# Row sums of 64 MB: two row blocks instead of four, a chained pair sum for the last row, and a first load of one row and of fifteen

## The chip, the cores and the metric

The kernel runs on one core of a Trainium2 chip. The metric is device time in microseconds (us). The kernel before takes 162.77 us (median of 3 runs, 162.54 to 163.09). Four names recur: SP (SyncE) only issues DMA transfers here, DVE (VectorE) and ACT (ScalarE) compute, and ACT also issues some stores. A transfer "lands" when its completion is signalled; a "packet" is one record of the profile for what one of the 16 DMA engines moved in one piece. The profiled span (from the first to the last instruction) is shorter than the device time by about 1.8 us: 161.3 us against 163.13 us for the same execution of the kernel before.

## The reference

```python
x = np.random.randn(32, 512, 1024).astype(np.float32)   # 67.1 MB
out = np.sum(x, axis=-1).astype(np.float32)             # 64 KB
```

That is 16,384 rows of 1024 numbers: each of the 128 partitions gets 128 rows.

## The kernel before

The rows are cut into four blocks; within a block a partition holds 32 consecutive rows, so neighbouring partitions lie 128 KB apart in memory (this distance is called the pitch below). SP issues loads of 16 rows per partition (8 MB, 64 KB in one run per partition) into three buffers. DVE reduces each buffer in one instruction. ACT issues a block's store as soon as its sums are there. The last 16 rows come in smaller loads and are shared between DVE and ACT.

```python
BLOCKS = (32, 32, 32, 32)
G = 16
ACT_ROWS = 6
CUT = 640
...
    xpool = ctx.enter_context(tc.tile_pool(name="x", bufs=3))
...
    for b, n in enumerate(BLOCKS):
        x_b, out_b, res = block(done * P, n)
        final = b == len(BLOCKS) - 1
        whole = n - G if final else n
        c = 0
        while c < whole:
            m = min(G, whole - c)
            xt = xpool.tile([P, G * D], F32, tag="xt", name="xt")
            nc.sync.dma_start(out=xt[:, 0 : m * D], in_=x_b[:, c * D : (c + m) * D])
            a = ACT_ROWS if done + c + m == full else 0
            rows_dve(xt, res, 0, m - a, c)             # one reduction over m - a rows
            rows_act(xt, res, m - a, a, c + m - a)     # one instruction per row
            c += m
        if not final:
            nc.scalar.dma_start(out=out_b, in_=res)    # the early stores
        done += n
    # the last 16 rows: loads of 8, 4, 2 and 1 rows, then the last row in two pieces
    ...
    nc.vector.tensor_reduce(
        out=tail[:, D : D + 1], in_=tail[:, 0 : CUT // 2], axis=X, op=ADD
    )
    sum_act(tail[:, CUT // 2 : CUT], tail[:, D + 1 : D + 2])
    nc.vector.tensor_reduce(
        out=res[:, n - 1 : n], in_=tail[:, CUT : D + 2], axis=X, op=ADD
    )
    nc.sync.dma_start(out=out_b, in_=res)
```

After compilation the first load is moved ahead of the barrier that opens the program. The whole kernel:

## Time and profile before

| | before |
|---|---|
| device time, median | 162.77 us |
| span of the profile | 161.3 us |
| DVE busy | 123.5 us (77%) |
| ACT busy | 15.8 us (10%) |
| bytes moved, mean rate | 67.18 MB, 416 GB/s |

The timeline of the kernel before; columns are start, duration (both us), engine, line, operation, output and input, and in brackets the idle time before it and what ended it. Each large reduction starts within 0.03 us of the landing of its load, so these starts are a list of the landings. "..." stands for lines left out. The line of 58.52 merges the three early stores, which are issued at 58.52, 97.26 and 136.55 us.

```profile
21.93 17.22 DVE L40 TENSOR_REDUCE res<-xt 128x16 f32<-128x16384 f32 x1 [21.93 <-DMA xt<-in_x_dram]
41.27 17.22 DVE L40 TENSOR_REDUCE res<-xt 128x16 f32<-128x16384 f32 x1 [2.13 <-DMA xt<-in_x_dram]
58.52 78.36 ACTq L82 DMA_DIRECT2D out_dram<-res  x3
60.64 17.22 DVE L40 TENSOR_REDUCE res<-xt 128x16 f32<-128x16384 f32 x1 [2.15 <-DMA xt<-in_x_dram]
80.01 17.22 DVE L40 TENSOR_REDUCE res<-xt 128x16 f32<-128x16384 f32 x1 [2.15 <-DMA xt<-in_x_dram]
99.57 17.22 DVE L40 TENSOR_REDUCE res<-xt 128x16 f32<-128x16384 f32 x1 [2.34 <-DMA xt<-in_x_dram]
...
119.30 17.22 DVE L40 TENSOR_REDUCE res<-xt 128x16 f32<-128x16384 f32 x1 [2.51 <-DMA xt<-in_x_dram]
...
138.73 18.46 DVE L40 TENSOR_REDUCE res<-xt 128x10 f32<-128x10240 f32 x4 [2.21 <-DMA xt<-in_x_dram]
...
157.95 0.47 ACT L48 ACTIVATE tail<-tail 128x320 f32<-128x320 f32 x1 [0.97 <-DMA tail<-in_x_dram]
157.95 0.49 DVE L102 TENSOR_REDUCE tail<-tail 128x1 f32<-128x320 f32 x1
...
158.55 0.55 DVE L106 TENSOR_REDUCE res<-tail 128x1 f32<-128x386 f32 x1
159.13 0.35 SPq L109 DMA_DIRECT2D out_dram<-res  x1
```

DVE is always done before the next load lands (17.22 us of work in 19.4 us), so the loads set the pace. Two of the distances between starts are longer than the others: 80.01 to 99.57 is 19.56 us and 99.57 to 119.30 is 19.73 us. At the end, ACT and DVE share the first piece of the last row (from 157.95); the last reduction adds ACT's part, DVE's part and the second piece.

### The profile page before, as it was taken

What the parts mean: (1) busy time and instruction counts of PE and PEld (TensorE: products, weight loads), DVE (VectorE), ACT (ScalarE), POOL (GpSimd) and SP (SyncE); (2) the same over time, 40 slices, a digit from 0 to 9 for tenths busy, and PEclk for the clock granted to TensorE, in tenths of its full rate; (3) what the DMA queues carried; (4) which work ended last, traced back from release to release, by engine and by line L of the source; (5) the groups of instructions that cost most, each with busy time, mean ns of one, the idle gap of its engine ahead of it and who ended that gap; (6) DMA issues with size and microseconds to landing.
All of it is one profiled execution on the core that took longest, in us unless ns stands there. A gap on an engine that the chain in (4) does not pass through costs nothing.

```text
span 161.3 us, 116 instructions
## 1 busy us (share of the span) xinstructions
DVE 123.5 (77%) x14; ACT 15.8 (10%) x29; POOL 0.2 (0%) x4
## 2 busy tenths in 40 slices
DVE  0000059997799959999499994999949998699994
ACT  0000000000000000000000000000000000891881
POOL 0000000000000000000000000000000000000000
DMA  7995995996995995996996996997979969999991
GB/s 260 520 520 260 520 520 260 520 520 260 520 520 260 520 520 260 521 521 260 521 520 260 520 520 260 521 456 326 521 309 471 520 260 520 390 391 449 406 407 44
DMA packets 2448, 67.18 MB, mean 416 GB/s; under 512 B 784, under 2 KB 912, under 8 KB 1168
## 3 DMA queue, kind: packets, MB, share of 16 engines
q1 hardware_dynamic: 2016, 67.13, 97.2%
q10 hardware_dynamic: 432, 0.05, 0.2%
HBM read 67.11 MB, written 0.07 MB: 416 GB/s over the span
## 4 chain that ended last, share of the span: by engine, by line
DMA 76%; DVE 22%; ACT 0%; issue 0%; ACTq 0%
DMA xt<-in_x_dram 39%; DMA tail<-in_x_dram 24%; DVE res L40 21%; DMA out_dram<-res 14%; DVE res L106 0%; ACT tail L48 0%; ACTq L115 0%
## 5 line engine op out<-in xcount | busy, mean ns | idle before, releaser
L40 DVE TENSOR_REDUCE res<-xt 128x16 f32<-128x16384 f32 (+4 forms) x10 | 121.8, 12203 | 35.4 <-DMA xt<-in_x_dram 35.4
L48 ACT ACT_TABLE_LOAD x1 | 1.3, 1283 | 137.0 <-DVE res L40 137.0
L48 ACT ACTIVATE xt<-xt 128x1024 f32<-128x1024 f32 x13 | 13.6, 1045 | 4.8 <-DMA xt<-in_x_dram 4.8
L48 ACT ACTIVATION_READ_ACCUMULATOR xt<-xt 128x1 f32 x13 | 2.4, 186 | 0.0
L56 DVE CUSTOM_DVE_ANT_0 xt<-xt 128x512 f32<-128x512 f32 x1 | 0.7, 692 | 0.0
L106 DVE TENSOR_REDUCE res<-tail 128x1 f32<-128x386 f32 x1 | 0.6, 554 | 0.1
L48 ACT ACTIVATE tail<-tail 128x320 f32<-128x320 f32 x1 | 0.5, 470 | 1.0 <-DMA tail<-in_x_dram 1.0
L102 DVE TENSOR_REDUCE tail<-tail 128x1 f32<-128x320 f32 x1 | 0.5, 486 | 0.0
L48 ACT ACTIVATION_READ_ACCUMULATOR tail<-tail 128x1 f32 x1 | 0.2, 187 | 0.0
L151 POOL MEMSET const-uint8-127<- 128x1 uint8 x1 | 0.1, 103 | 0.0
L151 POOL MEMSET const-bfloat16-1.0<- 128x1 bf16 x1 | 0.1, 102 | 0.0
L151 POOL MEMSET const-float32-0.0<- 128x1 f32 x1 | 0.1, 99 | 0.2 <-issue 0.2
L151 POOL MEMSET const-float32-1.0<- 128x1 f32 x1 | 0.1, 99 | 0.0
L56 DVE DVE_READ_ACCUMULATOR2_ANT res<- 128x1 f32 x1 | 0.1, 84 | 0.0
## 6 DMA issues: line engine op xcount, KB each, us to landing
xt<-in_x_dram SPq DMA_DIRECT2D x1, 4096.0 KB, 31.6
xt<-in_x_dram SPq DMA_DIRECT2D x1, 2048.0 KB, 36.1
xt<-in_x_dram SPq DMA_DIRECT2D x1, 1024.0 KB, 38.1
xt<-in_x_dram SPq DMA_DIRECT2D x1, 512.0 KB, 38.9
tail<-in_x_dram SPq DMA_DIRECT2D x1, 320.0 KB, 38.5
tail<-in_x_dram SPq DMA_DIRECT2D x1, 192.0 KB, 38.6
xt<-in_x_dram SPq DMA_DIRECT2D x7, 41.0
out_dram<-res ACTq DMA_DIRECT2D x3, 16.0 KB, 22.2
```

Source lines behind the costliest of these rows:

```text
L40: nc.vector.tensor_reduce(out=res[:, c : c + n], in_=xt[:, j * D : (j + n) * D].rearrange("p (j d) -> p j d", d=D), axis=X, op=ADD,)
L48: nc.scalar.activation(out=v, in_=v, func=COPY, accum_out=acc)
L56: nc.vector.tensor_tensor_reduce(out=xt[:, a:h], in0=xt[:, a:h], in1=xt[:, h:b], scale=1.0, scalar=first, op0=ADD, op1=ADD, accum_out=acc,)
L102: nc.vector.tensor_reduce(out=tail[:, D : D + 1], in_=tail[:, 0 : CUT // 2], axis=X, op=ADD)
L106: nc.vector.tensor_reduce(out=res[:, n - 1 : n], in_=tail[:, CUT : D + 2], axis=X, op=ADD)
L151: nc = _bacc.Bacc("TRN2", target_bir_lowering=False, num_devices=1)
```

## The change

The intent: fewer stores among the loads (two blocks, so one early store instead of three), a start-up in which a small load goes first, and an end in which DVE alone sums the last row, in two chained pair sums (an operation that adds the two halves of a piece and accumulates), the second of which starts from the first one's result. ACT takes one more whole row instead.

```diff
-BLOCKS = (32, 32, 32, 32)
+BLOCKS = (112, 16)
-CUT = 640
+CUT = 576
+EARLY = 2
...
-            nc.sync.dma_start(out=xt[:, 0 : m * D], in_=x_b[:, c * D : (c + m) * D])
+            parts = (0, 1, m) if done + c == 0 else (0, m)
+            for i, k in zip(parts, parts[1:]):
+                nc.sync.dma_start(
+                    out=xt[:, i * D : k * D], in_=x_b[:, (c + i) * D : (c + k) * D]
+                )
...
-    nc.vector.tensor_reduce(
-        out=tail[:, D : D + 1], in_=tail[:, 0 : CUT // 2], axis=X, op=ADD
-    )
-    sum_act(tail[:, CUT // 2 : CUT], tail[:, D + 1 : D + 2])
-    nc.vector.tensor_reduce(
-        out=res[:, n - 1 : n], in_=tail[:, CUT : D + 2], axis=X, op=ADD
-    )
+    rows_act(xt, res, 14, 1, c + 14)
+    pairs_dve(xt, last, last + CUT, 0.0, part)
+    pairs_dve(xt, last + CUT, last + D, part, res[:, c + 15 : c + 16])
...
-    load = next(i for i in code if i.engine == sp)
+    loads = [i for i in code if i.engine == sp][:EARLY]   # both go ahead of the barrier
```

Besides the number of stores, the blocks change two things: the early store has runs of 448 B instead of 128 B per partition, and neighbouring partitions of the first 112 rows lie 448 KB apart instead of 128 KB.

More of the change, by code (lines that the diff above doesn't have):

```diff
@@ L36, in row_sums @@
     rpool = ctx.enter_context(tc.tile_pool(name="res", bufs=1))
-    tail = rpool.tile([P, D + 2], F32, name="tail")
+    part = rpool.tile([P, 1], F32, name="part")
     def rows_dve(xt, res, j, n, c):
@@ L88, in row_sums @@
         nc.sync.dma_start(out=xt[:, i * D : k * D], in_=x_b[:, (c + i) * D : (c + k) * D])
-    last = (n - 1) * D
-    nc.sync.dma_start(out=tail[:, 0:CUT], in_=x_b[:, last : last + CUT])
-    nc.sync.dma_start(out=tail[:, CUT:D], in_=x_b[:, last + CUT : last + D])
-    for i, k in zip(cuts[:2], cuts[1:3]):
-        h = (k - i + 1) // 2
-        rows_dve(xt, res, i, h, c + i)
-        rows_act(xt, res, i + h, k - i - h, c + i + h)
-    i = cuts[2]
-    rows_dve(xt, res, i, 1, c + i)
-    rows_act(xt, res, i + 1, 1, c + i + 1)
-    i += 2
-    pairs_dve(xt, i * D, (i + 1) * D, 0.0, res[:, c + i : c + i + 1])
-    nc.vector.tensor_reduce(
-        out=tail[:, D : D + 1], in_=tail[:, 0 : CUT // 2], axis=X, op=ADD
-    )
-    sum_act(tail[:, CUT // 2 : CUT], tail[:, D + 1 : D + 2])
-    nc.vector.tensor_reduce(
-        out=res[:, n - 1 : n], in_=tail[:, CUT : D + 2], axis=X, op=ADD
-    )
+    last = 15 * D
+    for i, k in ((0, CUT), (CUT, D)):
+        nc.sync.dma_start(
+            out=xt[:, last + i : last + k],
+            in_=x_b[:, c * D + last + i : c * D + last + k],
+        )
+    for i, k in zip(cuts[:3], cuts[1:4]):
+        h = (k - i) // 2
+        rows_dve(xt, res, i, h, c + i)
+        rows_act(xt, res, i + h, h, c + i + h)
+    rows_act(xt, res, 14, 1, c + 14)
+    pairs_dve(xt, last, last + CUT, 0.0, part)
+    pairs_dve(xt, last + CUT, last + D, part, res[:, c + 15 : c + 16])
     nc.sync.dma_start(out=out_b, in_=res)
@@ L128 @@
     code = list(body.instructions)
-    load = next(i for i in code if i.engine == sp)
-    assert load.opcode == "DMACopy" and not load.sync_info.on_wait
-    code.remove(load)
+    loads = [i for i in code if i.engine == sp][:EARLY]
+    for load in loads:
+        assert load.opcode == "DMACopy" and not load.sync_info.on_wait
+        code.remove(load)
     body.instructions = code
@@ L134 @@
     at = next(k for k, i in enumerate(code) if i.engine == sp and i.opcode == "Drain")
-    code.insert(at, load)
+    code[at:at] = loads
     entry.instructions = code
```

## The prediction

> **What bounds the kernel before.** It is a stream of loads. The page gives 67.18 MB and no compute engine above 77% of the span (DVE 123.5 of 161.3 us). In the list of waits, DVE waits only for loads (35.4 us). In the timeline, DVE starts its seven large reductions at 21.93, 41.27, 60.64, 80.01, 99.57, 119.30 and 138.73 us, each time when a load lands, and then takes 17.22 us, less than the 19.4 us to the next landing. Single packet records show 64 KB per engine in 2.418 us, so 433.6 GB/s over 16 engines; the Trainium skill ("DMA: Bandwidth & Descriptors", "Where 436 GB/s comes from") puts the port ceiling at 435 GB/s, and the trace agrees. So only what is lost around it can shrink. Sixty-four such packets per engine are 154.8 us. First packets start at 0.99 us and the last load lands at 158.4: about 2.7 us are lost, of which the first packets take about 0.75 (3.2 us each instead of 2.42). After that landing come 0.12 us of waiting for ACT's part of the last row, a 0.55 us reduction, then store and closing (159.13 to 161.3).
>
> **What the change does.**
> 1. Three early stores of 128 B runs become one of 448 B runs. The undisturbed period between landings is 19.37 us; the periods with stores in flight are 19.56, 19.73 and 19.43, an excess of 0.6 us for somewhat over two stores, so 0.2 to 0.25 us each (an estimate). Two stores fewer: −0.45 us on the stream.
> 2. The partition stride of the loads goes from 128 KB to 448 KB. Runs stay 64 KB, and the engines already run at the port's rate: 0, with a small risk of a slower memory pattern.
> 3. First load 1 + 15 rows. The reduction stays one instruction over 16 rows, so DVE does not start earlier. The start-up loss is latency that small packets pay too: 0 to −0.4, I take −0.1[...].
> 4. Last row: DVE's reduction over 386 elements, after ACT (0.12 + 0.55 us after the landing), becomes a pair sum over 224 elements without ACT. From the 512-wide pair sum (0.69 us) I estimate about 0.40 us: −0.25.
> 5. A cost on ACT: its only early store now stands between its six rows and its last eight, and waits for DVE's ten-row reduction (10.82 us after the seventh landing), then takes 0.43 us. Eight rows at 1.04 us with a last read then end 19.7 us after the seventh landing, about when DVE's last pair sum ends. Before, ACT started these rows at 148.47, now about 149.4. So this nearly ties with the last landing and may eat 0 to 0.2 us.
>
> Sum: the last store is issued at about 158.4 instead of 159.13. The closing part is unchanged. **Predicted time 161.95 us**, range 161.3 to 162.6: 0.5% less. Chances: faster by over 2% 0.02, within 2% 0.96, slower 0.02.
>
> **What would show it.** Landing periods all close to 19.37 us up to the seventh; seventh landing near 138.1 instead of 138.7; ACT idle in the timeline until about 149 us with its rows then back to back; the last DVE operations about 0.4 us; the last wait shared between ACT's row and the last load.
>
> **What would make it wrong.** A 448 KB stride that slows packets above 2.42 us (slower by several us); a start-up loss that scales with the packet (up to 0.7 us more gain); an ACT tail that ends well after the last landing (up to 0.5 us less gain).

## More of the kernel before

Lines of the page of the kernel before: the span, busy time and its share, and the two DMA queues with packets, MB and the time of their packets as a share of 16 engines' span (q1 carries the loads and the last store, q10 the three early stores).

```profile
span 161.3 us, 116 instructions
...
DVE 123.5 (77%) x14; ACT 15.8 (10%) x29; POOL 0.2 (0%) x4
...
q1 hardware_dynamic: 2016, 67.13, 97.2%
q10 hardware_dynamic: 432, 0.05, 0.2%
```

The load queue takes 97.2% of what 16 engines have; no compute engine comes near.

## The result, and the profile after

| | before | after |
|---|---|---|
| device time, median | 162.66 us (4 runs, 162.46 to 163.09) | 162.32 us (4 runs, 162.26 to 162.56) |
| span of the profile | 161.3 us | 160.5 us |
| DVE, ACT busy | 123.5, 15.8 us | 122.7, 16.0 us |

The ratio after/before is 0.9979, with a 95% interval of 0.9955 to 1.0002. A ratio in this document is the mean time of one kernel's runs over that of the other's of the same rounds, so it isn't quite the ratio of the medians quoted; where a call had more runs of the kernel before than the rounds compared, the median quoted is that of all of them. The verdict is "same": a gain of 0.2%, where 0.5% was predicted.

Lines of the page of the changed kernel, as before:

```profile
span 160.5 us, 118 instructions
...
DVE 122.7 (76%) x14; ACT 16.0 (10%) x29; POOL 0.2 (0%) x4
...
q1 hardware_dynamic: 2160, 67.12, 97.3%
q10 hardware_dynamic: 144, 0.06, 0.1%
```

The timeline of the changed kernel, the lines that answer to those of before, and the early store with what follows it on ACT:

```profile
21.81 17.22 DVE L41 TENSOR_REDUCE res<-xt 128x16 f32<-128x16384 f32 x1 [21.81 <-DMA xt<-in_x_dram]
41.09 17.22 DVE L41 TENSOR_REDUCE res<-xt 128x16 f32<-128x16384 f32 x1 [2.06 <-DMA xt<-in_x_dram]
...
99.14 17.22 DVE L41 TENSOR_REDUCE res<-xt 128x16 f32<-128x16384 f32 x1 [2.13 <-DMA xt<-in_x_dram]
...
118.49 17.22 DVE L41 TENSOR_REDUCE res<-xt 128x16 f32<-128x16384 f32 x1 [2.13 <-DMA xt<-in_x_dram]
137.84 18.46 DVE L41 TENSOR_REDUCE res<-xt 128x10 f32<-128x10240 f32 x4 [2.13 <-DMA xt<-in_x_dram]
...
148.75 0.37 ACTq L87 DMA_DIRECT2D out_dram<-res  x1
149.25 1.06 ACT L49 ACTIVATE xt<-xt 128x1024 f32<-128x1024 f32 x1 [3.70 <-DVE res L41]
...
157.24 0.46 DVE L57 CUSTOM_DVE_ANT_0 xt<-xt 128x288 f32<-128x288 f32 x1 [0.93 <-DMA xt<-in_x_dram]
157.48 0.19 ACT L49 ACTIVATION_READ_ACCUMULATOR xt<-xt 128x1 f32 x1
...
157.77 0.45 DVE L57 CUSTOM_DVE_ANT_0 xt<-xt,part 128x224 f32<-128x224 f32 x1
...
158.29 0.35 SPq L108 DMA_DIRECT2D out_dram<-res  x1
```

At first sight this confirms the prediction handsomely. The distances between the starts from the second on are now all 19.35 us; the seventh load lands 0.89 us earlier (137.84 against 138.73), and the last store is issued 0.84 us earlier (158.29 against 159.13). But the timed runs moved by only 0.34 us, and the experiments show that three early stores can leave the periods unstretched and that periods stretch without any.

### The profile page after: what moved, and what is told of

Same layout as the page of the kernel before. It is cut to its first block, busy times and chain, and to the rows that moved or that the text cites. A ratio compares the mean times of both kernels' runs of the same rounds, so it can differ in the third digit from the quotient of the medians.

```text
span 160.5 us, 118 instructions
## 1 busy us (share of the span) xinstructions
DVE 122.7 (76%) x14; ACT 16.0 (10%) x29; POOL 0.2 (0%) x4
## 4 chain that ended last, share of the span: by engine, by line
DMA 74%; DVE 22%; SPq 1%; issue 0%; DVEq 0%
DMA xt<-in_x_dram 74%; DVE res L41 21%; SPq L93 1%; DVE xt L57 1%; DVEq L57 0%; DVE part L57 0%; DVEq L114 0%
## 5 line engine op out<-in xcount | busy, mean ns | idle before, releaser
L49 ACT ACTIVATE xt<-xt 128x1024 f32<-128x1024 f32 x14 | 14.6, 1042 | 3.7 <-DVE res L41 3.7
L57 DVE CUSTOM_DVE_ANT_0 xt<-xt 128x288 f32<-128x288 f32 x1 | 0.5, 459 | 0.9 <-DMA xt<-in_x_dram 0.9
L57 DVE CUSTOM_DVE_ANT_0 xt<-xt,part 128x224 f32<-128x224 f32 x1 | 0.5, 452 | 0.1
```

The lines of the kernel that those rows point to most:

```text
L49: nc.scalar.activation(out=v, in_=v, func=COPY, accum_out=acc)
L57: nc.vector.tensor_tensor_reduce(out=xt[:, a:h], in0=xt[:, a:h], in1=xt[:, h:b], scale=1.0, scalar=first, op0=ADD, op1=ADD, accum_out=acc,)
```

## The experiments

Twelve runs were made, each on one chip and beside its own runs of the kernel before. All gave the reference's result. Four numbers are read from each profile. "2nd" is the start of the second large reduction; "2nd to 7th" is the distance from there to the start of the seventh, five load periods in which the start-up and the end play no part. "7th to last load" leads on to the landing of the last load (from the semaphore events of the trace), and "to store" from there to the issue of the last store. "Long packets" counts the 64 KB packets of the loads that took over 2.45 us (their median is 2.418 to 2.42 us everywhere; there are 768 or 864 of them after the start).

| run | early stores | 2nd | 2nd to 7th | 7th to last load | to store | long packets | time / before | ratio (95%) |
|---|---|---|---|---|---|---|---|---|
| before | 3 x 128 B | 41.27 | 97.46 | 19.67 | 0.73 | 180 | - | - |
| f1_before_again | 3 x 128 B | 41.15 | 97.20 | 19.71 | 0.72 | 91 | 162.58 / 162.54 | 1.0004 (0.9991 to 1.0018) |
| e3_first_only | 3 x 128 B | 41.17 | 97.32 | 19.70 | 0.73 | 143 | 162.88 / 162.74 | 1.0009 (0.9994 to 1.0024) |
| e1_after_again | 1 x 448 B, late | 41.11 | 97.25 | 19.85 | 0.66 | 93 | 162.53 / 162.74 | 0.9991 (0.9977 to 1.0005) |
| e4_tail_only | 3 x 128 B | 41.31 | 96.81 | 19.67 | 0.66 | 5 | 162.51 / 162.74 | 0.9990 (0.9977 to 1.0003) |
| e5_three_stores | 128, 128, 192 B | 41.03 | 96.85 | 19.71 | 0.66 | 2 | 162.34 / 162.53 | 0.9983 (0.9970 to 0.9997) |
| e7_seven_stores | 7 x 64 B | 41.58 | 96.98 | 19.66 | 0.66 | 22 | 163.07 / 162.53 | 1.0029 (1.0016 to 1.0041) |
| after | 1 x 448 B, late | 41.09 | 96.75 | 19.79 | 0.66 | 16 | 162.32 / 162.66 | 0.9979 (0.9955 to 1.0002) |
| f3_after_third | 1 x 448 B, late | 41.39 | 96.75 | 19.76 | 0.66 | 15 | 162.31 / 162.54 | 0.9992 (0.9979 to 1.0004) |
| e2_blocks_only | 1 x 448 B, late | 41.25 | 96.76 | 19.77 | 0.73 | 9 | 162.58 / 162.74 | 0.9995 (0.9981 to 1.0008) |
| e6_one_block | none | 41.31 | 96.76 | 19.64 | 0.65 | 12 | 162.66 / 162.53 | 1.0002 (0.9989 to 1.0015) |
| e8_store_from_sp | none among the loads | 40.97 | 96.76 | 19.67 | 0.66 | 25 | 162.15 / 162.53 | 0.9978 (0.9962 to 0.9994) |
| f4_sp_store_again | none among the loads | 41.42 | 96.75 | 19.67 | 0.66 | 16 | 162.33 / 162.54 | 0.9989 (0.9976 to 1.0001) |
| f2_before_stores_last | none among the loads | 41.17 | 96.77 | 19.73 | 0.70 | 33 | 162.37 / 162.54 | 0.9997 (0.9985 to 1.0010) |

The theories were: A, the prediction's, that each store among the loads stretches the stream by 0.2 to 0.25 us; P, that the 448 KB pitch is what makes the stream quicker; B, that the stores cost nothing; and, after eight runs, S, that the stretched periods were a stretch of slower packets which comes and goes with the execution.

### e1: the changed kernel again

No edit.

> A repeat of the changed kernel, for the size of the noise and the repeat of its profile. Expected by my accounting: about 0.4 us less than the kernel before (ratio 0.997 to 0.999), seventh landing (the wait that frees the ten-row reduction) again near 137.8 us. If the gain is only chance between chips, the ratio is 1.000 and the landings move by several tenths.

The timed gain was smaller (ratio 0.9991), and the profile differs from the first one of the same kernel. The timeline of this run:

```profile
79.82 17.22 DVE L41 TENSOR_REDUCE res<-xt 128x16 f32<-128x16384 f32 x1 [2.14 <-DMA xt<-in_x_dram]
99.18 17.22 DVE L41 TENSOR_REDUCE res<-xt 128x16 f32<-128x16384 f32 x1 [2.14 <-DMA xt<-in_x_dram]
...
118.72 17.22 DVE L41 TENSOR_REDUCE res<-xt 128x16 f32<-128x16384 f32 x1 [2.32 <-DMA xt<-in_x_dram]
138.36 18.53 DVE L41 TENSOR_REDUCE res<-xt 128x10 f32<-128x10240 f32 x4 [2.42 <-DMA xt<-in_x_dram]
```

The distances are 19.36, 19.54 and 19.64 us, though this kernel's only early store is issued at 149 us, after all of them. So stretched periods arise without any store. The packet records show why: 93 packets of 64 KB took over 2.45 us, the longest 2.67 us, nearly all between 75 and 135 us; in the first profile of the same kernel it was 16, the longest 2.47 us. They are about enough to explain the stretch: between the second and the seventh reduction, what the long packets took beyond 2.418 us sums to 0.57 us per engine in e1, to 0.61 us in the kernel before, to 0.54 in e3 and 0.29 in f1, but to 0.09 us or less in every profile without such a stretch.

### e2, e3, e4: one part of the change at a time, in the kernel before

e2 has only the first hunk's blocks, e3 only the split first load and `EARLY = 2`, e4 only the pair sums and `CUT = 576`:

```diff
e2  -BLOCKS = (32, 32, 32, 32)
    +BLOCKS = (112, 16)
e3  +            parts = (0, 1, m) if done + c == 0 else (0, m)
    ...          (the loads of one and of fifteen rows, both ahead of the barrier)
e4  -    nc.vector.tensor_reduce(...)  sum_act(...)  nc.vector.tensor_reduce(...)
    +    rows_act(xt, res, 14, 1, c + 14)
    +    pairs_dve(xt, last, last + CUT, 0.0, part)
    +    pairs_dve(xt, last + CUT, last + D, part, res[:, c + 15 : c + 16])
```

> The kernel before with only the two blocks (112, 16). Theory A (stores cost the stream about 0.2 us each): landing periods after the first all 19.35 to 19.37 us, seventh landing about 0.6 us earlier than before (138.1), time about 0.4 us lower. Rival B (the stores cost nothing, the changed first load and tail bring the gain): seventh landing 138.7, time as before.

> The kernel before with only the first load split into one and fifteen rows ahead of the barrier. Theory A: first tile complete 0.1 to 0.2 us earlier (21.7 against 21.9), the later periods still stretched to 19.56 and 19.73, time 0.1 to 0.2 us lower. Rival B: 0.4 us lower.

> The kernel before with only the chained pair sums for the last row. Theory A, after the profile: from the last landing to the issue of the last store 0.66 us instead of 0.73, so 0.07 us lower and the time the same within noise. The prediction on record said 0.25 us lower. Rival: without the early gain of the stream, ACT's last rows no longer hold anything up and the full 0.25 us shows.

None of the three ratios is clear of 1. e2 has the quiet periods that theory A expected, but its ratio of 0.9995 is worth only 0.08 us, not 0.4. e4 refutes A outright: it has all three early stores, and no stretched period above 19.43 us. Its timeline:

```profile
60.66 17.22 DVE L40 TENSOR_REDUCE res<-xt 128x16 f32<-128x16384 f32 x1 [2.14 <-DMA xt<-in_x_dram]
80.09 17.22 DVE L40 TENSOR_REDUCE res<-xt 128x16 f32<-128x16384 f32 x1 [2.21 <-DMA xt<-in_x_dram]
99.38 17.22 DVE L40 TENSOR_REDUCE res<-xt 128x16 f32<-128x16384 f32 x1 [2.07 <-DMA xt<-in_x_dram]
...
118.80 17.22 DVE L40 TENSOR_REDUCE res<-xt 128x16 f32<-128x16384 f32 x1 [2.20 <-DMA xt<-in_x_dram]
...
138.12 18.47 DVE L40 TENSOR_REDUCE res<-xt 128x10 f32<-128x10240 f32 x4 [2.10 <-DMA xt<-in_x_dram]
```

The distances are 19.43, 19.29, 19.42 and 19.32 us. "2nd to 7th" is 96.81 us, against 96.75 to 96.77 in every quiet profile without early stores: two stores cost 0.04 to 0.06 us, so 0.02 to 0.03 each. For the tail, e4 gives 0.66 us from last landing to last store where the kernel before has 0.73; every profile with the pair sums has 0.65 or 0.66, and those with the old tail have 0.72 or 0.73 (0.70 in f2). That 0.07 us is the one part of the gain that repeats in every profile. e3 fell into a slow stretch (143 long packets) and its timed runs were not faster than before. Whether the split first load gains anything is not settled: the second reduction starts at 40.97 to 41.42 us in the profiles with the split first load at the 448 KB pitch and at 41.15 to 41.31 us in those without it. The packets hint at a shorter start. With one large load the first packets take 0.62 to 0.75 us more than the usual 2.418, on average over the engines. With the split, an engine's eight packets of 4 KB take 1.63 to 1.89 us instead of eight times 0.159, so 0.36 to 0.61 us more; e6 and e7, at other pitches, are left out here (0.09 and 0.50 us more, but their packets of 60 KB that follow lose another 0.32 and 0.34 us). That is an estimated 0.15 us between the averages, but the tile is complete when its slowest engine is, and there no difference shows.

### e5: three early stores in the changed kernel

```diff
-        if not final:
-            nc.scalar.dma_start(out=out_b, in_=res)
+            if not final and c in (32, 64, 112):
+                k = c - (48 if c == 112 else 32)
+                nc.scalar.dma_start(out=out_b[:, k:c], in_=res[:, k:c])
```

> The changed kernel, its one early store cut into three (columns 0 to 32, 32 to 64, 64 to 112) at the times when the kernel before stores; the partition pitch stays 448 KB. Theory A (each store in the stream costs 0.2 to 0.25 us): the periods in which stores are in flight stretch again to 19.55 to 19.75 us, seventh landing back by 0.4 to 0.6 us to 138.2 to 138.4, time 0.3 to 0.5 us above the changed kernel. Rival P (the 448 KB pitch gives the gain): periods stay 19.35, seventh landing 137.8, time unchanged.

Theory A fails again: 0.3 to 0.5 us were expected on top of the changed kernel, and the ratio to the kernel before is 0.9983, no worse than the changed kernel's 0.9979, 0.9991 and 0.9992. "2nd to 7th" is 96.85 us, 0.10 us over the quiet value for two stores, so 0.05 us each. (The packets of these two stores take 0.21 us per engine, twice what they cost; in e4 it is four times.) "7th to last load" is 19.71 us instead of 19.76 to 19.85: with a store of 192 B runs instead of 448 B the end is shorter. So for the changed kernel it is all the same whether one store or three leave early.

### e6 and e7: the pitch, and no early store or seven

```diff
e6  -BLOCKS = (112, 16)
    +BLOCKS = (128,)
e7  -BLOCKS = (112, 16)
    +BLOCKS = (16,) * 8
```

> The changed kernel with one block of 128 rows: no early store at all, one last store of 512 B runs, partition pitch 512 KB, a large power of two. Theory A: one store fewer in the stream, last landing 0.2 us earlier, last store 0.1 us longer: time 0 to 0.2 us below the changed kernel, packets still 2.42 us. Rival P (pitch matters): packets longer than 2.42 us and the time above by microseconds.

> The changed kernel with eight blocks of 16 rows: seven early stores of 64 B runs, six of them among the first seven loads; pitch 64 KB. Theory A: seventh landing later than in the changed kernel by 6 times 0.2 to 0.25 us, less what the last is still in flight, so 1.0 to 1.5 us, and the time higher by 1.2 to 1.5 us. Rival P: nothing moves that does not follow the pitch; if a smaller pitch is slower, all packets are longer.

The pitch between partitions is 512 KB in e6 and 64 KB in e7. In e6 "2nd to 7th" is 96.76 us, as at 128 KB without stores (f2, 96.77) and at 448 KB (96.75). So rival P falls: the pitch does not move the rate of this stream once it runs. Theory A's expectation for the time was missed too: 0 to 0.2 us below the changed kernel, but the five runs of e6 (162.41 to 162.76 us) all lie above those of e5 (162.26 to 162.37) on the same chip. In the profiles 0.28 us of that stands before the second reduction (41.31 against 41.03). Whether the pitch slows the start is not shown: f3 and f4 start as late (41.39 and 41.42) at 448 KB. The Trainium skill ("DMA: Bandwidth & Descriptors", "Latency and other measured facts") reports that copies between HBM tensors with a row pitch of 512 KiB reach only 207 GB/s per direction. This stream of loads into SBUF in 64 KB runs shows nothing of it, with 2.418 us per packet at 512 KB pitch, that is 433.6 GB/s. The case is not the same as the page's (loads, not copies between HBM tensors; longer runs).

e7 has five stores in flight between the second and the seventh reduction, and "2nd to 7th" is 96.98 us: 0.23 us more than without, so 0.05 us each, where theory A expected 1.0 to 1.5 us for six. Its queue line of the page, to be compared with q10 above:

```profile
q10 hardware_dynamic: 1008, 0.06, 0.4%
```

Its ratio of 1.0029 is worth 0.47 us, and it is the only one clearly above 1. The five stores explain 0.23 us of that at most. Its first load landed late as well (reduction at 22.30 us, elsewhere 21.69 to 22.14), and whether that belongs to the 64 KB pitch was not separated.

### e8 and f4: the early store behind all loads

SP issues the store after all its loads, so it stands in the same ring behind them, and ACT no longer waits.

```diff
-            nc.scalar.dma_start(out=out_b, in_=res)
+            held = out_b, res
...                                   # after the last load is issued
+    nc.sync.dma_start(out=held[0], in_=held[1])
```

> The changed kernel with its early store issued by SP after all loads instead of by ACT between its rows. Theory A (ACT's wait for the ten-row reduction is off the critical path, as its last row ends 0.6 us before the last store): ACT's eight last rows start about 147.5 us instead of 149.25, the last store is issued at the same 158.3 us, time unchanged. Rival (point 5 of the prediction: ACT nearly ties and eats up to 0.2 us): time lower by 0.1 to 0.2 us.

> The changed kernel with the early store issued by SP behind all loads, a second time. Theory S: from the seventh landing to the last load 19.69 us again instead of 19.8, as the 448 B runs (8 packets of 0.025 us per engine) no longer stand among the last loads: time 0.1 to 0.2 us below the changed kernel beside it, ratio to the kernel before 0.997 to 0.998. Rival: no difference between the two.

The timeline of e8, to be read against the end of the changed kernel above:

```profile
147.49 1.06 ACT L49 ACTIVATE xt<-xt 128x1024 f32<-128x1024 f32 x1 [2.05 <-issue]
...
148.61 0.35 SPq L101 DMA_DIRECT2D out_dram<-res  x1
...
157.54 0.45 DVE L57 CUSTOM_DVE_ANT_0 xt<-xt,part 128x224 f32<-128x224 f32 x1
...
158.06 0.34 SPq L110 DMA_DIRECT2D out_dram<-res  x1
```

ACT starts its last rows at 147.49 us, 1.76 us earlier than in the changed kernel, and the time from last landing to last store stays 0.66 us. So the wait of ACT for the ten-row reduction was off the critical path. It cost nothing: ACT had finished at 157.67 us in the changed kernel, 0.62 us before the last store. What did move is "7th to last load": 19.67 us in both e8 and f4, against 19.76 to 19.85 in the four profiles with the late 448 B store. So that one store, among the small last loads, costs about 0.1 us (0.09 to 0.12 in the three quiet profiles, 0.18 in e1). Its packets give an upper bound: each takes 0.025 us, eight per engine, about 0.2 us, where a 128 B packet takes 0.013 us.

In e8 the store issued at 148.61 us lands at 157.61, after the last load (157.40). The Trainium skill ("DMA: Bandwidth & Descriptors", "Queues, rings and completion order") says that an engine consumes one ring's descriptors in order and takes turns between rings packet by packet; the trace, whose packets do not name their engine, fits both. ACT's store at 58.52 us in the kernel before had its 128 B packets spread over the next 64 KB packets, about one per load packet, and landed at 82.40 us, 23.9 us later.

Timed, f4 is 0.05 us below f3 on the same chip (means 162.34 and 162.40), which is not clear of noise. e8 and f4 have ratios of 0.9978 and 0.9989 to the kernel before. This variant may be the quickest by a hair; of the two intervals only e8's is clear of 1, as e5's also is (0.9970 to 0.9997).

### f1, f2, f3: the kernel before, without its stores, and the changed kernel once more

f1 and f3 have no edit. f2 is the kernel before with its stores behind the loads:

```diff
-            nc.scalar.dma_start(out=out_b, in_=res)
+            held.append((out_b, res))
...                                   # after the last load is issued
+    for o, r in held:
+        nc.sync.dma_start(out=o, in_=r)
```

> A repeat of the kernel before, profiled once more. Theory S (the stretched periods of 19.56 and 19.73 us in its first profile were a stretch of slower packets that comes and goes with the execution): about half of such profiles are quiet; if this one is, all packets are near 2.42 us, each period with stores in flight is 19.37 to 19.43, seventh landing near 138.1 to 138.2. Rival A (stores stretch the periods by 0.2 to 0.25 us each): seventh landing 138.7 again with the same two periods stretched.

> The kernel before with its three early stores issued by SP behind all loads, so none in the load stream. Theory S (a store costs what its own packets take, about 0.05 us in the stream for 128 B runs): time 0.1 to 0.15 us below the kernel before, first quiet periods 19.35 us. Rival A: 0.6 to 0.7 us below, seventh landing 138.1 in every profile and no slow packets.

> The changed kernel a third time, to pool its ratio and to stand beside the next one on one chip. Theory S: ratio to the kernel before 0.998 to 0.999; its profile may or may not have slow packets.

The profile of f1 fell into a slow stretch again, but not the same one. Its timeline:

```profile
79.92 17.22 DVE L40 TENSOR_REDUCE res<-xt 128x16 f32<-128x16384 f32 x1 [2.20 <-DMA xt<-in_x_dram]
99.34 17.22 DVE L40 TENSOR_REDUCE res<-xt 128x16 f32<-128x16384 f32 x1 [2.20 <-DMA xt<-in_x_dram]
...
118.94 17.22 DVE L40 TENSOR_REDUCE res<-xt 128x16 f32<-128x16384 f32 x1 [2.37 <-DMA xt<-in_x_dram]
...
138.35 18.47 DVE L40 TENSOR_REDUCE res<-xt 128x10 f32<-128x10240 f32 x4 [2.20 <-DMA xt<-in_x_dram]
```

The period that ends at 99.34 us is 19.42 us (before: 19.56), the next 19.60 (before: 19.73); its seventh landing is 138.35, between the two that S and A named. So for the kernel before a quiet profile is still missing; e4 stands in for it, since its loads and early stores are those of the kernel before until the last row. f2 has a ratio of 0.9997, worth 0.05 us: less than the 0.1 to 0.15 us that S expected and not clear of 1, and far from the 0.6 to 0.7 us of A (its interval ends at 0.9985, worth 0.24 us). f3 repeats the quiet profile of the changed kernel and a ratio of 0.9992.

One thing stays open. The slow stretch appeared in four of the fourteen profiles: three of the six with several early stores among the loads, and one of the eight with one such store or none. So early stores are neither needed for it nor do they always bring it; whether they make it more likely can't be told from so few. What slows the packets in such a stretch no run here shows. The stretch is also not the only scatter: f3's profile is quiet, yet that execution took 162.56 us where three others took 162.28 to 162.31; its second reduction starts at 41.39 us, 0.30 us later than in the first profile of the same kernel. In e8 and f4, again one kernel, it starts 0.45 us apart (40.97 and 41.42).

## Why the prediction was right or wrong, point by point

The predicted time (161.95 us, range 161.3 to 162.6) held the measured 162.32 us, and "within 2%" was right. The size of the gain was not: 0.8 us from the sum, and measured were 0.34, 0.15 and 0.13 us in three comparisons (the ratios 0.9979, 0.9991 and 0.9992, times 162.7 us). Each of the three intervals just includes 1; weighted together by their widths (an estimate) they give 0.9990, 0.9981 to 0.9999, so a gain of about 0.16 us. That the time fell inside the range was partly luck: the largest term of the sum was wrong, and a gain of 0.15 us from the 162.77 us known at the time gives 162.62, just outside.

- **What bounds the kernel: right.** Every quiet profile has its load periods at 19.35 us whatever else is changed (19.29 to 19.43 with stores in flight), and a median packet of 2.418 or 2.42 us.
- **Point 1, stores "so 0.2 to 0.25 us each ... Two stores fewer: −0.45 us": this step failed.** The excess of 0.6 us in the profile before came from a stretch of slow packets (0.61 us per engine beyond the usual time). A store of 128 B runs costs 0.02 to 0.05 us (e4, e5; e7 with 64 B runs), and the one store of the changed kernel costs about 0.1 us where it stands. Three small stores and one large late one come to nearly the same: e5, with three, was no slower than the changed kernel.
- **Point 2, the pitch: right.** 448 KB and 512 KB give the same periods as 128 KB; at the start e6 leaves it open.
- **Point 3, the split first load, −0.1 us: not settled.** The packets' start-up is shorter on average over the engines, but the first tile is not reliably complete earlier.
- **Point 4, "−0.25" for the last row: mis-sized.** It is −0.07 us. The wait did not go, it changed its partner: before, the last operation started 0.15 us after the last landing (158.55 against 158.40) because ACT's part was awaited; now it starts 0.14 us after (157.77 against 157.63) because the first pair sum, itself waiting for its piece until 157.24, takes until then. And the second pair sum takes 0.45 us, not 0.40: hardly less than the 288-wide one (0.46), although it is 64 elements shorter.
- **Point 5, ACT's wait for its store "may eat 0 to 0.2 us": nothing was eaten.** ACT's rows started at 149.25 us as foreseen (149.4) and ended about 19.8 us after the seventh landing as foreseen (19.7); but DVE's pair sums ended 0.55 us later than ACT (158.22 against 157.67), and taking the wait away (e8) leaves the time from landing to store at 0.66 us.
- **"What would show it": a trap.** Even periods and an early seventh landing were named as signs of point 1. They appeared, and had another cause: e1, the same kernel, has two stretched periods and its seventh landing at 138.36. The stated risk of "a start-up loss that scales with the packet" did not come about.

The quiet profiles account for about 0.07 us (tail) plus at most some hundredths from the stores. What the measured 0.13 to 0.34 us have beyond that has no cause that these runs show; it is of the size of the scatter between executions.

## What to carry to other kernels

When one load stream sets the time and its packets all take the same time (here 2.418 us for 64 KB), bound the cost of a small store by the time of its own packets (the queue's share on the page: 0.2% of 161 us, about 0.3 us for three stores) and not by periods that happen to look longer while it is in flight. Here the packets' time was about two to five times what the stores cost. A profile is one execution: before a few tenths are given a cause, profile the unchanged kernel twice, and look whether the stretched part also appears in a variant that lacks the suspected cause. And where an operation waits for another engine, see what it would wait for next: taking ACT out of the last row gave only 0.07 us, as the chained pair sums brought a wait of the same length.

## What the Trainium skill lacked or had wrong

- No page tells of stretches of slower packets within a normal execution of a load stream. Here 64 KB packets took 2.45 to 2.67 us instead of 2.42 for tens of microseconds, in four of fourteen profiles, at a granted clock of 1.0, and made five load periods 0.4 to 0.65 us longer than in quiet profiles with the same stores. It belongs to "DMA: Bandwidth & Descriptors" (bandwidth), and to "Perfetto Trace Analysis" as a warning about single profiles.
- "DMA: Bandwidth & Descriptors" has no figure for a small store that runs beside a saturated load stream. Here a store of 128 runs of 128 B cost the stream 0.02 to 0.05 us, and one of 448 B runs among the small last loads about 0.1 us.
- The same page's warning about a 512 KiB row pitch (from copies between HBM tensors) does not say whether it holds for loads into SBUF. With runs of 64 KB at 512 KB pitch the packets took a median of 2.418 us after the start, the same as at other pitches.
- The same page gives a figure for the latency of the first byte, but not for what the start of a stream costs: the first 64 KB packets of the 16 engines took 0.62 to 0.75 us longer than later ones.
